# Nearest-neighbour upsampling by two: the rows of a partition taken from two blocks of the tensor instead of one

## The chip, the cores and the metric

The kernel runs on one core of a Trainium2 chip. The metric is the device time of one execution, in microseconds (us); lower is better. Before the change it is 197.49 us, the median of three runs (197.51, 197.10, 197.49).

The core's engines that matter here are VectorE (DVE in the profile) and ScalarE (ACT), which copy within the on-chip memory, SyncE (SP), which issues the transfers, and 16 DMA engines, which move data between the main memory (HBM) and the on-chip memory of 128 partitions. TensorE does nothing.

## The reference

`x` has the shape 16 x 64 x 64 x 64 in float32, 16.78 MB. Every element becomes a square of two by two in the output, 16 x 64 x 128 x 128 in float32, 67.11 MB:

```python
for i in range(new_h):
    for j in range(new_w):
        result[:, :, i, j] = x[:, :, i // 2, j // 2]
```

Batch, channel and height together make 65,536 input rows of 64 elements (256 B). One input row gives two output rows of 128 elements, which are neighbours in the output: 1024 B that are contiguous. So any run of input rows gives a contiguous run of output four times as long.

## The kernel before, in words

The 65,536 rows are dealt to the 128 partitions in one block: partition p owns rows 512p to 512p + 511 (`R` = 512). In `x` a partition's rows are 131,072 B, in the output 524,288 B, and these are the distances from one partition to the next.

All data lies in one on-chip tile, `mem`. Its upper part is `xt`, the whole input (512 rows a partition); below it is free space for 79 expanded rows. The input is fetched by three loads (line 194, cuts at rows 0, 256, 480 and 512), all issued at the start by SP. `begin_before_barrier` moves the first of them ahead of the barrier at the program's start.

Nine steps follow, of 52, 40, 52, 63, 52, 64, 63, 63 and 63 rows a partition. In each, DVE copies 9/16 of the step's rows in expanded form (line 214) and ACT the rest (line 215), both reading `xt` through an access pattern that repeats each element and each row, and then SP issues one store of the step's output (line 216). The expanded steps lie in turn at the bottom of `mem` and just below the rows of `xt` that are still needed, so a step's copies may begin when the store of the step before the last has landed. That is why the copies wait for stores.

The order on the queue is that of the program: three loads, then nine stores, all issued by SP in one queue. SP issues a store when the step's two copies are done. The first store has one wait more, set by hand: it waits for `loads[-2]`, the last load but one. Only the last load, of 32 rows, is then still under way. `close_early` rearranges the end of the program (the waits for the stores and the clearing of semaphores) and is the same in both kernels.

Of the kernel before, what the change touches and what calls it, by code (L numbers as in the profile page):

```python
# [153 lines left out]
@with_exitstack  # L154
def kernel(
    ctx: ExitStack,
    tc: tile.TileContext,
    x: bass.AP,
    scale_factor: int,
    out: bass.AP,  # L160
):
    nc = tc.nc
    nc.at_finalize(begin_before_barrier)
    nc.at_finalize(close_early)
    P = nc.NUM_PARTITIONS
    s = int(scale_factor)
    B, C, H, W = x.shape
    R = B * C * H // P
    fdt = x.dtype

    xp = x.rearrange("b c h w -> (b c h) w").rearrange("(p r) w -> p r w", p=P)
    op = out.rearrange("b c (h hd) w -> (b c h) (hd w)", hd=s).rearrange(
        "(p r) w -> p r w", p=P
    )

    rows = [52, 40, 52, 63, 52, 64, 63, 63, 63]
    GROW = s * s
    FREE = 79
    WF = FREE * GROW * W
    assert sum(rows) == R
    mem_pool = ctx.enter_context(tc.tile_pool(name="mem", bufs=1))
    mem = mem_pool.tile([P, WF + R * W], fdt, name="mem")
    xt = mem[:, WF:].rearrange("p (r w) -> p r w", r=R)

    cuts = [0, R // 2, R - 32, R]
    loads = [
        nc.sync.dma_start(out=xt[:, lo:hi], in_=xp[:, lo:hi])
        for lo, hi in zip(cuts, cuts[1:])
    ]

    def expanded(r0, r1):
        return (
            xt[:, r0:r1].unsqueeze(2).unsqueeze(4).to_broadcast([P, r1 - r0, s, W, s])  # L200
        )

    r0 = 0
    before = (0, 0)
    for n, k in enumerate(rows):
        size = k * GROW * W
        at = 0 if n % 2 == 0 else WF + r0 * W - size
        assert at >= before[1] or at + size <= before[0]
        before = (at, at + size)
        u = mem[:, at : at + size].rearrange(  # L210
            "p (k a w b) -> p k a w b", k=k, a=s, w=W
        )
        kv = k * 9 // 16
        nc.vector.tensor_copy(out=u[:, :kv], in_=expanded(r0, r0 + kv))  # L214
        nc.scalar.copy(out=u[:, kv:], in_=expanded(r0 + kv, r0 + k))  # L215
        store = nc.sync.dma_start(out=op[:, r0 : r0 + k, :], in_=u)  # L216
        if n == 0:
            tc.add_manual_dep(
                store.ins,
                loads[-2].ins.name,  # L220
                mybir.DependencyInfo(
                    mybir.DependencyClass.Sync, mybir.DependencyReason.DATA
                ),
                reason="stores begin as the loads end",
            )
        r0 += k
# [35 lines left out]
```

## Time and profile before

The profiled execution's span is 195.8 us (195.836 in the trace). Its own time is not recorded apart from its span; the median of the three runs is 197.49 us, that is 1.65 us more than the span, and this is taken for what lies around it.

| what | value |
|---|---|
| median of three runs | 197.49 us |
| span of the profiled execution | 195.8 us |
| what lies around the span, 197.49 - 195.84 | 1.65 us |
| DVE busy | 69.6 us (36%) in 9 copies |
| ACT busy | 51.4 us (26%), 9 copies and one table load |
| bytes read and written in HBM | 16.78 MB and 67.11 MB |
| rate over the span | 428 GB/s |

How to read it. An engine's share says how much of the span it was busy; here both copying engines idle for most of the time. The chain of work is the sequence of pieces, each released by the one ahead of it, that ended last. A DMA "issue" is the instruction with which SP hands a transfer to the queue, and "to landing" is the time from there until the last byte is in place; that includes the time in which the transfer stands behind others in the queue. A DMA packet is here one partition's contiguous piece of a transfer, moved by one of the 16 engines; a transfer over 128 partitions gives each engine eight data packets and one tiny packet that counts up the semaphore. The trace keeps one record of each packet (start, duration, bytes).

### The profile page before, as it was taken

How to read it: one execution, taken by the hardware profiler on the slowest of the kernel's cores; microseconds unless marked ns; L12 is line 12 of the kernel's file. 1: busy time of each engine (PE TensorE's matmuls, PEld its weight loads, DVE VectorE, ACT ScalarE, POOL GpSimd, SP SyncE). 2: the span in 40 equal slices, each digit the busy share in tenths (PEclk: the TensorE clock that was granted, in tenths of full speed). 3: DMA queues.
4: the chain of work that ended last, by engine and by line, in shares of the span. 5: the costliest groups of instructions: out<-in, count | busy, mean ns of one | idle time of the engine just before them, and what ended most of it. 6: DMA issues, size and time to landing. Idle time of an engine off the chain costs nothing.

```text
span 195.8 us, 102 instructions
## 1 busy us (share of the span) xinstructions
DVE 69.6 (36%) x9; ACT 51.4 (26%) x10; POOL 0.2 (0%) x4
## 2 busy tenths in 40 slices
DVE  0000596000039289069007205930693079100000
ACT  2000558000036083064920005666000074000000
POOL 0000000000000000000000000000000000000000
DMA  9999889699899999999999899999999999999994
GB/s 428 428 428 428 375 375 562 288 462 522 348 442 410 513 402 468 402 422 422 422 422 522 348 522 428 428 428 428 422 422 422 422 422 435 474 488 488 435 422 211
DMA packets 1728, 83.89 MB, mean 428 GB/s; under 512 B 192, under 2 KB 192, under 8 KB 192
## 3 DMA queue, kind: packets, MB, share of 16 engines
q1 hardware_dynamic: 1728, 83.89, 99.3%
HBM read 16.78 MB, written 67.11 MB: 428 GB/s over the span
## 4 chain that ended last, share of the span: by engine, by line
DMA 67%; DVE 18%; issue 0%; DVEq 0%; SPq 0%
DMA out_dram<-mem 48%; DMA mem<-in_x_dram 19%; DVE mem L214 18%; DVEq L214 0%; SPq L216 0%
## 5 line engine op out<-in xcount | busy, mean ns | idle before, releaser
L214 DVE COPY mem<-mem 128x8960 f32<-128x8960 f32 (+3 forms) x9 | 69.6, 7738 | 97.8 <-DMA out_dram<-mem 75.9
L215 ACT COPY mem<-mem 128x7168 f32<-128x7168 f32 (+2 forms) x9 | 50.1, 5572 | 111.7 <-DMA out_dram<-mem 82.7
L215 ACT ACT_TABLE_LOAD x1 | 1.3, 1283 | 0.8 <-PEq L243 0.8
L243 POOL MEMSET const-bfloat16-1.0<- 128x1 bf16 x1 | 0.1, 101 | 0.0
L243 POOL MEMSET const-uint8-127<- 128x1 uint8 x1 | 0.1, 101 | 0.0
L243 POOL MEMSET const-float32-0.0<- 128x1 f32 x1 | 0.1, 98 | 0.2 <-issue 0.2
L243 POOL MEMSET const-float32-1.0<- 128x1 f32 x1 | 0.1, 98 | 0.0
## 6 DMA issues: line engine op xcount, KB each, us to landing
out_dram<-mem SPq DMA_DIRECT2D x4, 8064.0 KB, 28.4
out_dram<-mem SPq DMA_DIRECT2D x3, 6656.0 KB, 19.7
mem<-in_x_dram SPq DMA_DIRECT2D x1, 7168.0 KB, 38.0
out_dram<-mem SPq DMA_DIRECT2D x1, 5120.0 KB, 29.7
mem<-in_x_dram SPq DMA_DIRECT2D x1, 1024.0 KB, 40.1
mem<-in_x_dram SPq DMA_DIRECT2D x1, 21.8
out_dram<-mem SPq DMA_DIRECT2D x1, 29.9
```

The lines of the kernel that those rows point to most:

```text
L214: nc.vector.tensor_copy(out=u[:, :kv], in_=expanded(r0, r0 + kv))
L215: nc.scalar.copy(out=u[:, kv:], in_=expanded(r0 + kv, r0 + k))
L243: nc = _bacc.Bacc("TRN2", target_bir_lowering=False, num_devices=1)
```

## The change

The rows are dealt in two blocks. The first 128 x 207 rows of `x` form the first: partition p owns rows 207p to 207p + 206 of it. The remaining 128 x 305 rows form the second: partition p owns 305 of them, one after another. 207 is the sum of the first four steps (52 + 40 + 52 + 63), so no step crosses the seam. The distance between partitions becomes 52,992 B in `x` and 211,968 B in the output in the first block, and 78,080 B and 312,320 B in the second.

The loads are cut at the seam. There are four of them, of 207, 256, 17 and 32 rows a partition, where there were three of 256, 224 and 32. The nine steps, their sizes, their places in `mem` and the shapes of the copies stay. The first store still waits for `loads[-2]`, which is now the load of 17 rows.

```diff
-    xp = x.rearrange("b c h w -> (b c h) w").rearrange("(p r) w -> p r w", p=P)
-    op = out.rearrange("b c (h hd) w -> (b c h) (hd w)", hd=s).rearrange(
-        "(p r) w -> p r w", p=P
-    )
+    A = 207
+    xf = x.rearrange("b c h w -> (b c h) w")
+    of = out.rearrange("b c (h hd) w -> (b c h) (hd w)", hd=s)
+
+    def owned(flat, lo, hi):
+        a, b = (0, A) if hi <= A else (A, R)
+        assert a <= lo < hi <= b
+        block = flat[P * a : P * b].rearrange("(p r) w -> p r w", p=P)
+        return block[:, lo - a : hi - a]
...
-    cuts = [0, R // 2, R - 32, R]
+    cuts = [0, A, A + 256, R - 32, R]
     loads = [
-        nc.sync.dma_start(out=xt[:, lo:hi], in_=xp[:, lo:hi])
+        nc.sync.dma_start(out=xt[:, lo:hi], in_=owned(xf, lo, hi))
         for lo, hi in zip(cuts, cuts[1:])
     ]
...
-        store = nc.sync.dma_start(out=op[:, r0 : r0 + k, :], in_=u)
+        store = nc.sync.dma_start(out=owned(of, r0, r0 + k), in_=u)
```

## The prediction, made before the changed kernel was timed

> **What bounds the kernel now.** I read the page's DMA part first, because the two copying engines are busy for only 36% and 26% of the span.
>
> ```profile
> GB/s 428 428 428 428 375 375 562 288 462 522 348 442 410 513 402 468 402 422 422 422 422 522 348 522 428 428 428 428 422 422 422 422 422 435 474 488 488 435 422 211
> ...
> q1 hardware_dynamic: 1728, 83.89, 99.3%
> ```
>
> One queue, and its packets fill 99.3% of the time of 16 DMA engines. The rate swings from slice to slice, which looks like idle stretches but is a matter of counting: a slice is 4.9 us and two of the largest packets fill it, so whole packets fall into one slice or the next. The trace's packet records settle it. No view prints them, so I tell them: followed engine by engine, each engine moves 5.24 MB without a gap of more than 3 ns from its first packet to its last. A packet of 65,536 B takes 2418 ns, one of 64,512 B 2380 ns, of 57,344 B 2116 ns and of 8192 B 309 ns, loads and stores alike. 16 x 65,536 B / 2418 ns is 433.7 GB/s, and 506 of the 512 packets of 64,512 B took 2380 ns exactly. Equal times to the nanosecond for reads and writes at different addresses mean a fixed pace of the engine, not a memory that is sometimes busy.
>
> Second, the DMA issues, to see whether there is always work in the queue:
>
> ```profile
> out_dram<-mem SPq DMA_DIRECT2D x4, 8064.0 KB, 28.4
> out_dram<-mem SPq DMA_DIRECT2D x3, 6656.0 KB, 19.7
> mem<-in_x_dram SPq DMA_DIRECT2D x1, 7168.0 KB, 38.0
> ```
>
> A store of 8064 KB is eight packets of 2380 ns an engine, 19.0 us, yet it lands 28.4 us after its issue: it stood 9.4 us behind others. Third, the chain of waits, where the loads give way to the stores:
>
> ```profile
> 0.79 37.97 DMA mem<-in_x_dram
> 38.77 0.02 issue
> 38.78 0.03 SPq L216
> 38.81 0.05 issue
> 38.86 18.12 DMA out_dram<-mem
> 56.98 0.03 issue
> 57.00 0.02 DVEq L214
> 57.02 0.05 issue
> 57.07 7.90 DVE mem L214
> 64.97 0.02 issue
> 64.99 0.02 SPq L216
> 65.00 0.03 issue
> 65.03 19.69 DMA out_dram<-mem
> ```
>
> The chain names DVE for 18% of the span, but its 7.90 us are hidden: the third store is issued at 65.03 us, and by the packet records the engines are busy with the second one until 68.49 us at the earliest. From the first issue (0.00) to the first packet it took 1.40 us, so 3.46 - 1.40 = 2.06 us of slack remain at this place; every later store is issued at least 5.4 us before the queue runs dry. So **the time is the queue's start, plus the bytes at the engines' pace, plus 1.65 us around the span**: the slowest engine's first packet starts at 1.86 us and ends at 4.96 us, and 190.87 us of back-to-back packets follow to 195.84 us.
>
> **The change part by part.**
>
> *The copies.* Nothing is added or removed: nine on DVE and nine on ACT with the same shapes in the same order. The first load is 49 rows shorter, 12,544 B less in each of an engine's eight packets. The pace per byte is (2412 - 306) / 57,344 = 0.0367 ns (starts of neighbouring packets of 65,536 and 8192 B lie 2412 and 306 ns apart), so it lands 8 x 12,544 x 0.0367 = 3.7 us sooner, near 18.2 instead of 21.86 us. Steps 0 and 1 end 3.7 us sooner (30.2 instead of 33.9 us). Worth nothing: their store is held until `loads[-2]` lands at 38.8 us. If the copies were late instead, they could be so by 4.9 us before it.
>
> *The order of bytes.* Before the gate the queue carries 256 + 224 = 480 rows, after it 207 + 256 + 17 = 480. The gate opens at the same point of the stream, with the same 32-row load as cover.
>
> *One load more.* SP issues four instead of three: each took 0.33 to 0.42 us on SP, all done by 2.0 us, while the first load keeps the engines busy to 18 us. Hidden. On the DMA engines each gets eight data packets and one semaphore packet more. A packet's fixed part is 306 - 8192 x 0.0367 = 5.4 ns, the semaphore packet 6 ns. So 8 x 5.4 + 6 = 49 ns, **+0.05 us**, all of it on the path because the engines never idle. Lower bound 0.03 us (8 x 3 ns, the smallest step between packets, and 6). The upper bound for packets of 4352 B, half as long as any data packet in this trace, is that each still takes the 306 ns of 8192 B instead of 5.4 + 160 = 165: 8 x 141 ns = 1.1 us more. I take 0.05, since packets of five sizes lie on one line. A page of the Trainium skill speaks against such a transfer: "DMA: Bandwidth & Descriptors", under "Anatomy of one DMA", fits 2.0 us of fixed cost and bytes at 436 GB/s to each DMA (of GpSimd's path), and "Rules for kernel authors" asks for at least 1 MiB, which 17 rows (0.56 MB) miss; taken as time on the path it would give about 199.5 us. This trace shows that the fixed part isn't paid between queued transfers: the 32-row load of 1 MB occupied an engine for 2.45 us, eight packets of 306 ns, with its neighbours within 6 ns.
>
> *The gate's wait.* It now ends when the 17-row load lands. Behind it on SP stand all the stores. Before, it opened at 38.78 us, the store was issued at 38.86, and at 1.40 us from issue to packet the queue has new work at 40.26. The earliest engine runs dry at 40.68 us (its last 32-row packet's end), so 0.42 us are left over. The cost is zero as long as a small transfer's landing is signalled within 0.4 us of what a large one's is. Above that every us counts once.
>
> *The addresses.* Packets stay contiguous, on 256 B, and as long as before; only the distance between partitions changes, from powers of two to 207 and 305 KiB in the output and a quarter of that in `x`. No run here shows such distances. From below: a packet cannot beat the pace of 2380 ns if that is the engine's own, as equal times for loads and stores at distances of 128 and 512 KiB say; so no gain on queued packets. From above: the slowest of 512 packets took 2466 ns; if all stores went at that, 3.6% of their 155 us, +5.6 us. I take 0, the row of 506 in 512. The page named above, under "Latency and other measured facts", reports copies between HBM tensors at 207 GB/s with a row pitch of 512 KiB and 214 with a padded pitch, so by it the stores would gain 3%, about 5 us, and end near 192.5 us; the packets at 433.7 GB/s leave no room for it.
>
> *The first packets.* They are the one place where memory shows: 3022 to 3387 ns instead of 2418, 0.6 to 0.97 us more. With the new distances this may vanish (-0.97 at most) or grow by the same spread (+0.37). I take 0: a cold start, which has nothing ahead of it to hide its first read.
>
> **Sum.** 195.84 + 0.05 = 195.89 us of span; with 1.65 us around it 197.54 us, against a median of 197.49.
>
> **The rivals.**
>
> *The new distances make packets collide (slower).* Place: the stores, where 16 engines write in lockstep; the loads had 37 of the 196 us. For it: six of 512 packets did wait, up to 86 ns, so there is something to wait for. Against: the other 506 did not, at distances which, as powers of two, are the likeliest to meet. Price: 1.55 us for every 1% on 155 us of stores; between nothing and 3.6% I price it at 1%, 199.1 us. It decides from 6 ns a packet (0.25%, 0.39 us).
>
> *The cover at the gate fails (slower).* If the 17-row load is signalled a full 1.40 us late, 1.40 - 0.42 = 1.0 us of idle engines follows, 198.5 us. For it: only 0.42 us of slack. Against: where I compared them, a landing follows its last packet within 0.05 us (second load: both at 38.78 us; first store: 56.94 and 56.98 us).
>
> *The start gets shorter (faster).* The engines' first reads at 128 KiB distances wait for each other; at 52,992 B they don't. The first packets' excess of 0.6 to 0.97 us goes, 197.54 - 0.75 = 196.8 us. Against: the excess is on all 16 engines alike, also the one that starts first, which looks like a plain latency.
>
> *Nothing at all.* The extra packets may cost nothing visible; 197.49 us is inside my forecast.
>
> **How the numbers follow.** What a measurement of this kernel can tell from no change is about 0.2%, 0.4 us; the three runs spread over 0.41 us. Forecast, no difference (197.1 to 197.9 us): 0.79. Faster start: 0.10. Collisions: 0.07. Gate: 0.04. So faster 0.10, same 0.79, slower 0.11. The range goes from 197.0 us, most of the way to the faster start, to 198.2 us, which takes in about half of the gate's price, the runs' own spread, and half of the 1.1 us bound on small packets; the tail of the collisions (up to 203.1 us) is in the part left out.
>
> **What would show it.** Right: data packets of unchanged duration by size, the 17-row load's packets near 168 ns, the queue near 99.3%, first copies at about 18.2 us, first store's issue near 38.9 us and no engine idle at 40.7 us. Wrong: store packets above 2380 ns (collisions), a gap between the last load packet and the first store packet (gate), or first packets well under 3.0 us beyond their 0.46 us fewer bytes (start).

## The result and the profile after

The changed kernel took 197.74 us (median of 10 runs, 197.70 to 198.03); beside it the kernel before took 197.35 us (10 runs, 197.06 to 197.51). The ratio is 1.0025, with a 95% interval of 1.0017 to 1.0033: slower by a quarter of a per cent. The time lies inside the forecast range, 0.20 us from the forecast, and inside the 197.1 to 197.9 us of "no difference", the case with 0.79. But against the kernel before, measured beside it, the ratio is just past the 0.2% that I had drawn as the bound of what can be told from no change.

The profiled execution has a span of 196.7 us, 0.86 us more than before. It is one of two of the ten runs near 198.0 us; the other eight took 197.70 to 197.78 us with spans of 196.4 us. In all these runs the time is 1.3 to 1.4 us more than the span, so the profiled execution of before, with its span of 195.84 us, must have been one near 197.2 us, below its median. So the two profiles stand 0.86 us apart where the medians are 0.39 us apart.

The page of the changed kernel, its rows on the transfers:

```profile
span 196.7 us, 102 instructions
...
DMA  8999999799899999999999899999999999999994
GB/s 334 474 399 466 426 440 453 317 450 509 357 440 400 519 401 466 401 420 420 420 420 520 347 520 426 426 426 426 420 420 420 420 420 525 459 433 433 459 420 210
DMA packets 1872, 83.89 MB, mean 426 GB/s; under 512 B 208, under 2 KB 208, under 8 KB 336
...
q1 hardware_dynamic: 1872, 83.89, 99.0%
...
mem<-in_x_dram SPq DMA_DIRECT2D x1, 6624.0 KB, 19.0
```

The packet count is 144 higher, the 128 data packets and 16 semaphore packets of the fourth load. The busy share is 99.0% and not 99.3%. The first load lands at 19.0 us, where I had 18.2: it is already 0.8 us late. The chain of waits at the change from loads to stores (start, duration, what) says the same of the gate:

```profile
1.18 38.50 DMA mem<-in_x_dram
39.67 0.02 issue
39.69 0.03 SPq L222
39.72 0.05 issue
39.76 18.09 DMA out_dram<-mem
57.85 0.03 issue
57.88 0.02 DVEq L220
57.90 0.05 issue
57.95 7.90 DVE mem L220
```

The first store is issued at 39.76 us and not at 38.86; all that follows is moved by that 0.9 us. From there the two chains run alike: the first store's 18.09 us were 18.12 us, and the copy after it takes 7.90 us as before.

The trace's packet records, followed engine by engine, show where the 0.9 us come from. Packet times in this document, as in the prediction, are counted so that an execution's last packet ends with its span. On the trace's own clock, which is that of the issues and landings in the chains, every packet is earlier by a fixed amount: 0.39 us before, 0.37 us after, 0.36 to 0.44 us in the other runs. Durations, gaps and spreads are the same on both. In the table, the excess of a first packet is its duration less the usual one of its size (2418 ns for 65,536 B, 1956 ns for 52,992 B). The mean gap is what an engine lay idle between its last load packet and its first store packet. The packet of 64,512 B stands for the stores, as the mean over the four stores that have it.

| | before | after |
|---|---|---|
| first packets start, us | 1.40 to 1.86 | 1.38 to 2.48 |
| excess of the first packet, us | 0.60 to 0.97 | 0.18 to 1.84 |
| last of the first packets ends, us | 4.96 | 5.33 |
| engines end their loads, us | 40.68 to 41.24 | 40.68 to 42.09 |
| mean gap ahead of the first store, us | 0.003 | 0.18 |
| packet of 64,512 B, ns | 2380 | 2386 |

One engine's first packet took 3798 ns and kept that engine late to the end of the loads: from the end of its first packet it needed 36.77 us, no more than the others (36.77 to 36.93 us). The gate (the first store's wait) waits for the slowest engine, most of the others run dry in the meantime (they have no packet left to move), and the stores' packets are afterwards a few ns longer. I had priced longer store packets as a matter of the stores' addresses. That, the loads' addresses and the fourth load were told apart by experiment.

### The profile page after: what moved, and what is told of

Its sections match the earlier page's. It is cut to its first block, busy times and chain, and to the rows that moved or that the text cites. A ratio compares the mean times of both kernels' runs of the same rounds, so it can differ in the third digit from the quotient of the medians.

```text
span 196.7 us, 102 instructions
## 1 busy us (share of the span) xinstructions
DVE 69.6 (35%) x9; ACT 51.4 (26%) x10; POOL 0.2 (0%) x4
## 4 chain that ended last, share of the span: by engine, by line
DMA 67%; DVE 18%; issue 0%; SPq 0%; DVEq 0%
DMA out_dram<-mem 47%; DMA mem<-in_x_dram 20%; DVE mem L220 18%; SPq L200 0%; DVEq L220 0%; SPq L222 0%
```

## The experiments

Each ratio is against the kernel before, run on the same chip, with its 95% interval. What is said of packets comes from one profiled execution of each kernel.

**The fourth load alone.**

```diff
-    cuts = [0, R // 2, R - 32, R]
+    cuts = [0, 207, 463, R - 32, R]
```

> One block of 512 rows as before, loads and stores at the addresses of before, but four loads, cut at rows 207, 463 and 480 as in the changed kernel. Theory S (the two-block addresses of the stores make each store packet 4 to 7 ns longer, about 72 packets an engine, +0.4 us): nothing but the 0.05 us of the additional load, ratio about 1.000, store packets of 64,512 B at 2380 ns. Theory L (the two-block addresses of the loads make the first packets uneven, so that the slowest engine enters the stores 0.85 us late): also about 1.000, and the slowest engine begins its stores near 41.3 us. Theory G (the fourth load itself, through SP's issue and the first store's wait for a small transfer): ratio about 1.002, with gaps ahead of the first store.

Measured: 1.0011 (1.0002 to 1.0020). The loads ended at 40.80 to 41.23 us, the mean gap was 3 ns, the 64,512 B packets took 2380 to 2381 ns. About 0.2 us in the medians (197.38 against 197.19), of which the additional packets explain 0.05; the profiled run's span, 195.9 us, shows hardly more than that. So theory G's mechanism, a gap ahead of the first store, is not there.

**The stores' addresses alone** (`owned` and `of` as in the change).

```diff
-        store = nc.sync.dma_start(out=op[:, r0 : r0 + k, :], in_=u)
+        store = nc.sync.dma_start(out=owned(of, r0, r0 + k), in_=u)
```

> The three loads and the x addresses of before; only the stores go to the two-block addresses, so that rows land in other places than the reference has them, while sizes and counts are the same. Theory S: ratio 1.002 to 1.0025, store packets of 64,512 B with a mean of 2385 to 2387 ns instead of 2380, span near 196.3 us. Theories L and G: ratio 1.000, packets at 2380 ns.

Measured: 0.9999 (0.9990 to 1.0008), packets at 2380 to 2381 ns. Theory S falls: the two-block output costs nothing.

**The loads alone** (the converse of the last edit: `owned` for the four loads, `op` as before for the stores).

> The four loads of the changed kernel from the two-block addresses of x; the stores go to the one-block addresses of before, so that rows land in other places than the reference has them. Theory S: ratio about 1.000 to 1.0005, store packets at 2380 ns. Theory L: ratio 1.002 or more, slowest engine's stores begin near 42 us instead of 41.2. Theory G: ratio 1.002, with gaps of 0.1 to 0.4 us on most engines ahead of the first store.

Measured: 1.0032 (1.0020 to 1.0045). The largest excess of a first packet was 1.51 us, the slowest engine ended its loads at 41.71 us, the mean gap was 0.10 us. Yet the stores, at the addresses of before, had 64,512 B packets of 2383 to 2386 ns. So the longer packets come with the loads' addresses, two steps further on. Theory L takes the whole loss.

**The gate opened earlier.**

```diff
-                loads[-2].ins.name,
+                loads[-3].ins.name,
```

> The changed kernel, but the first store waits for the load of 256 rows (the last but two) and not for that of 17, so 49 rows instead of 32 stand in the queue as cover, 1.4 us more. Theory S: still 1.002 to 1.0025 above the kernel before, gaps at the first store gone. Theory G: ratio 1.000 to 1.0005. Theory L: ratio 1.002, since the slowest engine has no gap at this place.

Measured: 1.0061 (1.0049 to 1.0074), which no theory had. The first store was issued at 37.97 us, and the store packets ran at 2380 ns. But from 39.8 us on, that is 1.5 us after that issue on the trace's own clock, packets of 8192 B that took 309 ns before took up to 856 ns, and the slowest engine ended its loads at 42.31 us. A store that was queued this early slowed the loads still under way. That is a price of a larger cover which my rivals did not have.

**Which load it is.** The one-block kernel with four loads, and only the first load's rows taken from another distance:

```diff
+    first = xf[: P * 207].rearrange("(p r) w -> p r w", p=P)
...
-        nc.sync.dma_start(out=xt[:, lo:hi], in_=xp[:, lo:hi])
+        nc.sync.dma_start(out=xt[:, lo:hi], in_=(first if lo == 0 else xp)[:, lo:hi])
```

> The one-block kernel with four loads, but the first load (207 rows a partition) reads from rows 207 apart, 52,992 B, as in the changed kernel, instead of 512 apart; all other loads and all stores at the addresses of before, so that the first 207 rows of a partition are other rows than the reference's. Theory F (the first load's addresses make the first packets uneven): ratio 1.002 to 1.003, the slowest engine ends its loads at 41.5 to 42.1 us instead of 41.24. Rival R (the later loads' addresses do it): ratio about 1.001, as the one-block kernel with four loads had, loads ended by 41.25 us.

Measured: 1.0036 (1.0023 to 1.0048), the loads ended by 41.65 us, the largest excess was 1.41 us. The complement, only the three later loads moved (`rest[:, lo - 207 : hi - 207]` for them):

> The complement of e5_first_load_207: the first load reads at the addresses of before, the three later ones from rows 305 apart in the second block, as in the changed kernel; stores as before, so that rows 207 to 511 of a partition are other rows than the reference's. Theory F: ratio about 1.001, loads ended by 41.3 us, first packets of at most 0.85 us over their pace. Rival R: ratio 1.002 to 1.003 and loads ended at 41.5 us or later.

Measured: 1.0010 (1.0001 to 1.0018), loads ended by 41.26 us, largest excess 0.90 us: the same as the four loads without any new address. Theory F holds, R falls. The chain of the first of these two kernels shows the step in a one-block kernel of which only the first load was changed:

```profile
1.16 38.04 DMA mem<-in_x_dram
39.20 0.02 issue
39.22 0.03 SPq L218
39.25 0.05 issue
39.30 18.14 DMA out_dram<-mem
```

The first store goes out at 39.30 us against 38.86.

**Which property of the distance.** Three more values in place of 207:

> As the run named e5_first_load_207, but the first load reads from rows 256 apart, 65,536 B, a power of two (again other rows than the reference's). If theory F holds and it is the odd distance that hurts: ratio about 1.001 and loads ended by 41.3 us. If it is the small distance (partitions lying close together) that hurts: ratio 1.002 to 1.003, loads ended at 41.5 us or later. Rival R: about 1.001 in either case.

> As the run named e5_first_load_207, but the first load reads from rows 208 apart, 53,248 B, a multiple of 4 KiB (other rows than the reference's). If the fine alignment of the odd distance matters: ratio about 1.001 and loads ended by 41.3 us. If any distance near 52 KB does it: ratio 1.003 or more, loads ended at 41.5 us or later.

> As the run named e5_first_load_207, but the first load reads from rows 511 apart, 130,816 B: an odd number of rows, yet nearly the distance of before (other rows than the reference's). If it is a distance off the power of two that makes first packets uneven: ratio 1.003 or more, loads ended at 41.5 us or later. If it is partitions lying close together: ratio about 1.001, loads ended by 41.3 us.

| rows between partitions, first load | ratio (95%) | largest excess, us | loads ended by, us |
|---|---|---|---|
| 512 (four loads, as above) | 1.0011 (1.0002 to 1.0020) | 0.84 | 41.23 |
| 256 | 1.0015 (1.0006 to 1.0024) | 0.86 | 41.42 |
| 207 | 1.0036 (1.0023 to 1.0048) | 1.41 | 41.65 |
| 208 | 1.0028 (1.0017 to 1.0040) | 1.60 | 41.83 |
| 511 | 1.0043 (1.0030 to 1.0056) | 0.63 | 42.00 |

Of the five values the two powers of two are the fast ones. 256 rows came out a little above what I expected (1.001, 41.3 us), and its interval overlaps that of 208, but no run of the two overlaps: 197.28 to 197.68 us at 256 rows and 197.69 to 197.98 us at 208, with a median of 197.17 us for the kernel before beside each. Neither closeness (256 is nearly as close as 208) nor alignment to 4 KiB (208 has it) is the cause. 511 loses in another way than 207: its first packets are good, but from about the fifth packet of the first load on there are gaps of some tenths of a us, and the packets of the second load, whose addresses are those of before, took 2445 ns in the mean instead of 2418. What makes a distance good was not found, nor whether it takes a power of two: another multiple of 64 KiB, such as 384 rows, was not run.

**Does running dry cost more than the gap?** The kernel before, with the gate on the last load:

```diff
-                loads[-2].ins.name,
+                loads[-1].ins.name,
```

> The kernel before with one edit: the first store waits for the last load (32 rows), so that every engine runs dry ahead of the first store. Store issue near 41.3 us, first store packets from about 42.6 us, a gap of 1.3 to 2.0 us on every engine. Theory D (an engine that ran dry here goes on at about 7 ns more a packet): the store phase takes 155.05 to 155.15 us on every engine instead of 154.59, ratio 1.009 to 1.012. Rival (the slower store packets of the changed kernel belong to its loads' addresses and not to the gap): store phase 154.59 us, ratio 1.007 to 1.009.

Measured: 1.055 (1.0536 to 1.0565). The edit did more than I meant: the second step's store (5120 KB) was issued at 33.91 us, ahead of the first one's at 42.23 us. The copies of the third step then began only at 70.10 us, and the queue stood empty from 70 to 79 us. The page shows it as slices of 134 and 0 GB/s, and the early store by its 20.5 us to landing:

```profile
GB/s 406 406 406 406 533 355 499 257 487 381 457 495 361 134 0 330 495 495 400 400 400 400 495 495 330 406 609 406 403 400 400 400 587 412 400 400 400 400 599 200
...
q1 hardware_dynamic: 1728, 83.89, 94.7%
...
out_dram<-mem SPq DMA_DIRECT2D x1, 5120.0 KB, 20.5
```

So it is no clean test of the gate, but it bears on the question: at unchanged addresses, store packets of 53,248 B took 1966 ns before the gap, and after it 1973 to 1977 ns; those of 64,512 B, all after it, took 2384 to 2389 ns (means of one store each). Here too a store stood in the queue well before the loads ended, and 61 of the 128 packets of the last load took more than their 309 ns, up to 804. The clean form has a last load of 8 rows, with the second store held like the first, so that the order stays:

```diff
-    cuts = [0, R // 2, R - 32, R]
+    cuts = [0, R // 2, R - 8, R]
...
-        if n == 0:
+        if n < 2:
```

> The one-block kernel before with a last load of 8 rows instead of 32 (the second has 248), the second store holding the same wait as the first so that the order of the stores stays. The wait ends near 40.6 us, the first store packets come at 41.9 to 42.5 us, and every engine runs dry by 0.7 to 1.8 us. Theory D: every store phase takes about 155.1 us, span 197.4 to 197.6 us, ratio 1.008 to 1.009. Rival (running dry costs only the gap): store phases of 154.6 us, span 196.9 to 197.1 us, ratio 1.005 to 1.0065.

Measured: 1.0072 (1.0060 to 1.0085), span 197.3 us. Its chain at the gate:

```profile
0.78 39.92 DMA mem<-in_x_dram
40.70 0.02 issue
40.72 0.03 SPq L216
40.75 0.05 issue
40.80 17.17 DMA out_dram<-mem
```

The store is issued at 40.80 us. On the trace's own clock the engines end their loads between 0.48 us before that and 0.19 us after it, and the first store packets come 0.84 to 0.99 us after it (42.02 to 42.17 us as the table counts), a mean gap of 1.17 us. All 16 engines then took 155.06 to 155.14 us for the stores, where 154.59 us was the rule before. Theory D's phase holds, in a kernel with no new address; its ratio came out a little below what I expected, since no gap was over 1.5 us, where I had up to 1.8. The ratio alone does not tell it from the rival; the store phases do.

**The dry engines fed again, in the changed kernel.**

```diff
-    cuts = [0, A, A + 256, R - 32, R]
+    cuts = [0, A, A + 256, R - 40, R]
```

> The changed kernel with the last load of 40 rows instead of 32 (and the third of 9 instead of 17), so that the first store's wait ends some 0.6 us earlier in the stream of loads. Theory D (engines that ran dry at the gate go on at 5 to 7 ns more a packet, and this adds to the uneven start): few engines run dry, most store phases are 154.6 us, and the end is set by the slowest engine alone, 41.5 to 42.1 + 154.6 = 196.1 to 196.7 us of span, so a ratio of 1.000 to 1.002 when the changed kernel has 1.0025. Rival (the slowest engine's late start sets the end in any case): the same ratio as the changed kernel, 1.002 to 1.003. Second rival (the first store's own start disturbs loads still under way, as when the wait was moved to the 256-row load): 1.004 or more, with packets of 8192 B above 309 ns.

Measured: 1.0039 (1.0027 to 1.0052). No engine ran dry (mean gap 2 ns), and nearly all store phases were 154.59 us, the longest 154.74; 64,512 B packets took 2380 ns again. Still the time is no better than the changed kernel's: the slowest engine ended its loads at 41.88 us and the kernel at 196.5 us, 41.88 + 154.59. Eight of the 128 packets of the last load took 392 to 732 ns instead of 385. Six of the eight lie on the four engines that were latest, which they made later by up to 0.35 us. Without them the loads would have ended near 41.63 us, by the largest end of a first packet (4.86 us) and the 36.77 us that undisturbed engines need from there. So both rivals of this expectation have a part in the time: the late engine sets the end, and the earlier store made the late engines later. What the dry engines alone cost the changed kernel this run cannot tell, since the larger cover took back what it may have gained.

No version here beats the kernel before.

## Why the prediction was right or wrong

*What bounds the kernel*: right. In every run but the one with the misordered stores, the end is an engine's loads' end plus 154.6 to 154.9 us of stores, or plus up to 155.1 us and a gap where it ran dry. One thing beneath it was misread. I set the packets' times beside issues and landings without seeing that they were 0.39 us late against them: on the trace's own clock the first packet starts 1.01 us after the first issue, not 1.40, and a landing follows its last packet by 0.34 to 0.42 us, not by under 0.05. The slacks of 0.42 and 2.06 us stand, because the two errors cancel in them.

*The copies*: right, worth nothing, with the same 7.90 us in the chain. Only the time of the first landing was off (19.0, not 18.2 us), for the reason below.

*One load more*: the packets of 4352 B took 168 ns, as forecast, so the 0.05 us on the engines stands. The run with nothing else changed lost 0.0011 (0.0002 to 0.0020), which holds 0.05 us (0.0003) but has its middle at 0.2 us. The rest is not placed.

*The addresses of the stores*: right at zero, and now shown (0.9999). The reason that the trace gave, a fixed pace of the engine, was stronger than the slower packets that I had kept as the upper bound. After the change the store packets were longer, which I had named as the sign of collisions; that sign would have misled, since the cause lay ahead of the stores. The Trainium skill, in "DMA: Bandwidth & Descriptors", under "Latency and other measured facts", gives copies between HBM tensors a slightly lower rate at a row pitch of 512 KiB (207 GB/s) than at a padded one (214). For stores from the on-chip memory this case shows no such gain: they gained nothing by leaving 512 KiB, and the first load lost by leaving its power of two, 128 KiB.

*The first packets*: this is the step that failed. I bounded them by -0.97 and +0.37 us and took 0, as a plain latency that any address would have. The runs show an excess that depends on the distance: its largest value was 0.84 to 1.06 us in the seven profiled executions with 512 or 256 rows, and 1.36 to 1.84 us in the six with 207 or 208. In the profiled execution that engine's first packet ended at 5.33 instead of 4.96 us while being 0.46 us shorter: 0.82 us late, and with the 0.05 us of additional packets that is, to 0.02 us, its 42.09 against 41.24 us at the end of the loads. I had put a chance of 0.10 on this term getting smaller and none on its getting larger. My rivals for "slower" were the stores and the signalling of a small load; neither is what happened.

*The gate*: "the gate opens at the same point of the stream" was right for the count of rows and wrong for the time. The slack of 0.42 us that I worked out holds for engines that stay within 0.55 us of each other. With a spread of 1.41 us the gate, which waits for the slowest, came too late for the fastest. So the cover failed, by skew and not by a late signal: the 17-row load landed 0.41 us after its last data packet, the load that held the gate before 0.37 us. In the profiled execution the last of the dry engines ended 0.01 us after the late one, which itself had no gap and 154.6 us of stores. In the run with the loads alone it was 0.11 us, in the one with 208 rows 0.22 us. So the late engine explains most of the loss, and running dry can add to it.

*The sum*: 197.54 us forecast, 197.74 measured beside 197.35 for before (197.49 in the forecast's reference), so the change of +0.05 us was in fact +0.39 us. That the time came so near is in part luck: the reference, a median of three, stood 0.14 us above the median of ten. The 1.65 us around the span was also too large. In every run that lists both, the time is 1.28 to 1.38 us more than the span; the rest of the 1.65 us was the difference between the profiled execution and the median. It did no harm, since the sum adds back what was taken off. And the loads had 39 us of the span, from 1.40 to about 41 us, not the 37 that the first rival puts.

What stays open: how the 0.39 us divide between the late engine and the dry ones in the usual execution, why distances that are not powers of two upset the first load, why 511 rows do it later and differently, and why an engine that ran dry needs 5 to 7 ns more for each later packet.

## What to carry to other kernels

Where the trace showed transfers back to back at one fixed pace, new addresses cost nothing: not the stores (0.9999) and not the later loads (1.0010, as with the fourth load alone). The first transfer of a program is another matter: nothing hides its latency, and the slowest of the 16 engines kept its lateness to the end. At 511 rows even the later packets of that first load, and the load behind it, lost time. A wait on a whole transfer is a wait on its slowest engine, so its slack must be reckoned with the spread among engines and not from their mean. A longer packet in a late stage is a symptom that may belong to an earlier one; it takes runs that change one stage at a time to say which.

## What the runs showed of the hardware that I had not expected

- Engines that ran dry ahead of a store went on at 2384 to 2389 ns for each packet of 64,512 B, and not 2380, for the remaining 125 to 155 us, about 0.5 us in all; this was so in one-block and in two-block kernels, after gaps of 0.2 us (mean) and of 9 us.
- A store issued too early slows the loads that are still under way: 8192 B packets took up to 856 ns instead of 309 with the gate on the 256-row load, and up to 804 with the misordered stores. The cover of 32 rows at a spread of 0.55 us left no gap and no slowed packet.
- The distance between partitions in the first load matters (powers of two 1.0011 and 1.0015, others 1.0028 to 1.0043), while that in the stores does not (0.9999).
